# A decoder block on one core: products of the first up pair among those of the first gate pair, two products split by token tiles, and earlier loads in the down projection

## The chip, the core and the metric

The kernel runs on one core of a Trainium2 chip (trn2). The metric is the device time of one execution in microseconds, the median of the runs. Engines are named as in the profile: PE is TensorE's matmuls, PEld its weight loads, DVE is VectorE, ACT is ScalarE, POOL is GpSimd, and SP is SyncE, whose queue issues nearly all DMAs here.

## What is computed

One layer on 1024 tokens of width 1024: RMS norm, one input projection, a retention head group and a differential-attention head group, an output projection, and a SwiGLU feed-forward of width 2816. The change touches the part from the output projection on, which is:

```python
mix = jnp.concatenate([ret, dif.astype(ret.dtype)], axis=-1)
x = x + jnp.einsum('bse,ed->bsd', mix, w_out[l]).astype(x.dtype)

h2 = rms_norm(x, norm2_g[l])
ff = jax.nn.silu(jnp.einsum('bsd,df->bsf', h2, w_gate[l])) * jnp.einsum('bsd,df->bsf', h2, w_up[l])
x = x + jnp.einsum('bsf,fd->bsd', ff, w_down[l]).astype(x.dtype)
```

All in float32. To keep the precision, each product of two matrices is made of three matmuls on split operands: hi x hi, hi x lo and lo x hi, where hi is a value rounded to fp32r and lo is the rest (`mm3`).

## The kernel before

**Before the part in question.** Attention and retention run in steps over head groups and token tiles of 128, then the output projection (`o_proj`) of a token tile t and a half dh of the width, eight matmul triples each.

**The middle (`mid`, lines 1196 to 1216).** Thirteen output projections are still to be made (`PAIRS`), 104 steps of one triple, and then the first pair of gate columns, seven products of four steps each. In front of a pinned loop stands `MID_PLAN`, a list of (step, function, arguments) written out by hand: after a step's matmuls the functions of that step are called, and each engine runs its instructions in just that order. So MID_PLAN is the order of DVE, ACT and POOL in this stretch; PE's own order is that of the steps with the transposes between.

For each token tile t and half q of the width these functions follow one another:
- `o_add` (DVE) adds the projection to x, and SP stores the row to `x2d`; `n_square` (ACT) squares it with a sum; `n_rs` (POOL) makes the norm's factor; `n_scale` (DVE) scales the row in place; `n_turn` (PE) transposes it; `n_back` (ACT) copies it back, `n_hi` (ACT) and `n_lo` (DVE) split it.
- `f_sum` (DVE), `f_hi` (ACT), `f_lo` (DVE) make the sums and differences of such rows and split them.

The feed-forward's products are Strassen's: seven products n of quarter matrices in place of eight. The operand of product n from the tokens is a block `blk[b]` of four token tiles, and the seven products take b = 0, 3, 1, 4, 2, 5, 6 in this order. Block 0 holds tiles 0 to 3 of the first half of the width, block 3 the difference of the halves for them; block 1 holds tiles 4 to 7 of the second half, block 4 their difference, and 2, 5 and 6 mix both groups of tiles. `f_sum(b, p)` makes tile p of block b. So products 2 and 3 need token tile 7, the last one to come out of the output projection, as p = 3, and 4, 5 and 6 need all tiles.

The operand from the weights is `w_sum` (POOL, where the product takes a sum), `w_hi` (ACT) and `w_lo` (DVE), out of two raw halves that `Strassen.__init__` loads (tag rawp, three buffers, one of which holds the norm's gain `gtile` until the last `n_scale`). The first gate pair has these written into MID_PLAN as `gw_sum`, `gw_hi`, `gw_lo`; its results go out by `g_first` (ACT) and `g_more` (DVE). A product's bank in PSUM comes from three kinds, pp (two), m (two) and h (four), by `next_bank`.

**After the middle** nothing is pinned by hand: a scheduler sets the order of the up pair of the same columns and of ten more gate and up pairs. Each pair's planes go to DRAM (`ffd`, `plane`).

**The down projection** makes seven products n over 11 columns c. For each c it loads a plane into a ring of eight buffers (`a_load`), splits it and a weight (`operand`), and issues twelve matmuls, three into each of four banks. At the end of a product DVE adds the four banks to `acc` tiles, which `STARTS` loads from `x2d`: before the change in the last four columns of products 0 to 2, those of the half dh = 0 into the pool rowa, those of dh = 1 into rowb. rowa also holds the up results of the last pair until their planes are made, which `LAST` places at columns 3 to 7 of product 0.

In the notation below, g0 to g6 are the products of the first gate pair and u0 to u6 those of the first up pair.

Of the kernel before, what the change touches and what calls it, by code (L numbers as in the profile page):

```python
# [52 lines left out]
def constants():  # L53
# [69 lines left out]
    (0, "n_square", 1, 0),  # L123
# [6 lines left out]
    (1, "n_square", 0, 0),  # L130
# [97 lines left out]
    (80, "f_sum", 4, 1),  # L228
    (81, "o_add", 6, 0),
    (81, "f_hi", 4, 1),  # L230
    (82, "o_load", 7, 0),
    (82, "n_square", 6, 0),
    (82, "f_lo", 4, 1),
    (83, "n_lo", 5),
    (88, "o_add", 6, 1),
    (89, "gw_sum", 0),
    (89, "o_load", 7, 1),
    (89, "n_square", 6, 1),
    (90, "gw_hi", 0),
    (90, "n_rs", 6),  # L240
    (91, "gw_hi", 1),
    (91, "gw_lo", 0),
    (92, "gw_hi", 3),
    (92, "n_scale", 6, 0),
    (93, "gw_lo", 1),
    (94, "n_scale", 6, 1),
    (94, "n_turn", 6, 0),
    (95, "gw_lo", 3),
    (95, "n_back", 6, 0),
    (95, "n_turn", 6, 1),  # L250
    (95, "gw_sum", 2),
# [3 lines left out]
    (97, "f_sum", 4, 2),
    (98, "n_square", 7, 0),
    (98, "gw_lo", 2),
    (99, "gw_sum", 4),
    (99, "n_hi", 6),
    (100, "f_hi", 4, 2),  # L260
    (100, "n_lo", 6),
    (101, "gw_hi", 4),
    (101, "f_lo", 4, 2),
    (102, "gw_lo", 4),
    (103, "f_sum", 2, 0),
    (104, "gw_sum", 5),
# [1079 lines left out]
```

## Time and profile before

| | us |
|---|---|
| median of 3 runs | 1228.01 (1226.68 to 1230.36) |
| the profiled execution | 1226.93 |
| its span | 1225.1 |
| PE busy | 1204.8 |
| DVE busy | 838.1 |
| POOL busy | 570.8 |
| ACT busy | 537.2 |

The middle begins at about 503 us and the gate pair in it at 579.56; the down projection begins after 1005. A row of the timeline has the start, the time taken, the engine, the line, the operation with what it writes and reads, the shape, how many were merged, and in brackets the idle time of the engine before it with what ended it. Tile names come without numbers: in this stretch `x` is a token tile's row, `act` a block or the projection's operand, `whi` and `wlo` the weights' parts, `c` a result, `wide` a buffer of the down projection. All instructions of the pinned engines have the line of the helper, L347. A row of windows has the stretch, its length, the busy time and count of PE, PEld, DVE, ACT and POOL, the granted clock, the share of the DMA engines and GB/s.

### The profile page before, as it was taken

How to read it: one execution, taken by the hardware profiler on the slowest of the kernel's cores; microseconds unless marked ns; L12 is line 12 of the kernel's file. 1: busy time of each engine (PE TensorE's matmuls, PEld its weight loads, DVE VectorE, ACT ScalarE, POOL GpSimd, SP SyncE). 2: the span in 40 equal slices, each digit the busy share in tenths (PEclk: the TensorE clock that was granted, in tenths of full speed). 3: DMA queues.
4: the chain of work that ended last, by engine and by line, in shares of the span. 5: the costliest groups of instructions: out<-in, count | busy, mean ns of one | idle time of the engine just before them, and what ended most of it. 6: DMA issues, size and time to landing. Idle time of an engine off the chain costs nothing. (4 is left out here: it accounts for less than half of the span.)

```text
span 1225.1 us, 17316 instructions
## 1 busy us (share of the span) xinstructions
PE 1204.8 (98%) x5944; PEld 1020.6 (83%) x5944; DVE 838.1 (68%) x1491; ACT 537.2 (44%) x1194; POOL 570.8 (47%) x719
## 2 busy tenths in 40 slices
PE   8999999999999999999899999999999999999998
PEld 7898989888888888787688888888888888788887
DVE  6988888854444445545997665757657659698697
ACT  6856666643222224434544344333443434344442
POOL 2656555644444443102276456545566536154053
PEclk9999999999999999999999999999999999999999
DMA  6201011102111111422233333323334177943342
GB/s 201 67 21 32 27 30 35 44 17 88 52 35 40 39 35 45 154 84 72 60 122 119 95 103 112 128 71 103 104 112 129 69 254 247 349 144 99 95 116 83
DMA packets 97383, 117.34 MB, mean 96 GB/s; under 512 B 8976, under 2 KB 60304, under 8 KB 97296
## 3 DMA queue, kind: packets, MB, share of 16 engines
q1 hardware_dynamic: 95968, 115.65, 29.5%
q8 instruction: 47, 0.77, 0.3%
q10 hardware_dynamic: 1328, 0.60, 0.3%
q14 instruction: 40, 0.33, 0.1%
HBM read 87.64 MB, written 28.57 MB: 95 GB/s over the span
## 5 line engine op out<-in xcount | busy, mean ns | idle before, releaser
L347 PE MATMUL pp<-whi,act 128*128 128x384 f32 (+1 forms) x896 | 287.8, 373 | 0.7 <-ACT whi L347 0.7
L347 POOL TENSOR_TENSOR sum<-rawp 128x512 f32<-128x512 f32 x110 | 157.2, 1430 | 174.5 <-DVE wlo L347 152.6
L347 ACT CAST whi<-sum 128x512 fp32r<-128x512 f32 x165 | 102.6, 622 | 204.9 <-PE h L347 62.8
L347 DVE TENSOR_TENSOR wlo<-sum,whi 128x512 fp32r<-128x512 f32 x165 | 167.7, 1016 | 34.0 <-ACT whi L347 33.5
L347 PE MATMUL h<-act,whi 128*128 128x512 f32 x608 | 187.5, 389 | 0.3 <-DVE act L347 0.3
L347 PEld LDWEIGHTS pp<-whi,act 128*128 128x128 f32 x896 | 167.4, 189 | 15.2 <-ACT whi L347 1.0
L347 PE MATMUL pp<-wlo,act 128*128 128x384 f32 (+1 forms) x448 | 161.6, 361 | 0.6 <-DVE wlo L347 0.6
L347 POOL TENSOR_TENSOR sum<-wide 128x512 f32<-128x512 f32 x55 | 85.7, 1560 | 134.0 <-DVE wlo L347 101.9
L347 PEld LDWEIGHTS h<-act,whi 128*128 128x128 f32 x608 | 114.1, 188 | 24.5 <-DVE act L347 0.7
L347 PE MATMUL pp<-wrh,act 128*128 128x512 f32 x384 | 130.7, 402 | 0.0
L347 PE MATMUL h<-act,wlo 128*128 128x512 f32 x304 | 118.3, 389 | 0.0
L347 DVE TENSOR_TENSOR wlo<-wide,whi 128x512 fp32r<-128x512 f32 x99 | 78.5, 816 | 32.5 <-ACT whi L347 32.5
L347 PE MATMUL m<-act,whi 128*128 128x512 f32 x312 | 97.7, 394 | 1.8 <-ACT act L347 1.2
L347 ACT CAST whi<-wide 128x512 fp32r<-128x512 f32 x99 | 59.3, 620 | 87.3 <-PE m L347 48.0
L347 PE MATMUL pp<-act,whi 128*128 128x512 f32 x312 | 96.4, 390 | 0.7 <-DVE act L347 0.7
L347 PEld LDWEIGHTS pp<-wlo,act 128*128 128x128 f32 x448 | 85.1, 190 | 7.6 <-DVE wlo L347 1.2
L347 POOL TENSOR_TENSOR fsum<-c 128x512 f32<-128x512 f32 x55 | 79.2, 1451 | 11.0 <-DMA ffd<-fsum 11.0
L347 PEld LDWEIGHTS pp<-wrh,act 128*128 128x128 f32 x384 | 72.2, 188 | 14.3
L347 DVE TENSOR_TENSOR c<-c,h 128x512 f32<-128x512 f32 x88 | 58.1, 682 | 32.6 <-PE h L347 32.5
L347 DVE TENSOR_TENSOR wlo<-rawp,whi 128x512 fp32r<-128x512 f32 x44 | 47.4, 1077 | 41.1 <-ACT whi L347 40.2
L347 PE MATMUL pp<-wrl,act 128*128 128x512 f32 x192 | 74.8, 390 | 0.0
L347 PEld LDWEIGHTS m<-act,whi 128*128 128x128 f32 x312 | 59.2, 190 | 14.6 <-ACT act L347 1.4
(162 smaller groups left out, 2515.7 us busy)
## 6 DMA issues: line engine op xcount, KB each, us to landing
wide<-ffd SPq DMA_DIRECT2D x77, 256.0 KB, 2.7
ffd<-fsum SPq DMA_DIRECT2D x55, 256.0 KB, 2.0
rawp<-in_w_gate_dram SPq DMA_DIRECT2D x22, 512.0 KB, 3.8
rawp<-in_w_up_dram SPq DMA_DIRECT2D x22, 512.0 KB, 3.9
wide<-in_w_down_dram SPq DMA_DIRECT2D x44, 256.0 KB, 5.3
raw<-in_w_in_dram SPq DMA_DIRECT2D x32, 256.0 KB, 2.8
ffd<-c SPq DMA_DIRECT2D x22, 256.0 KB, 2.0
raw<-in_w_in_dram SPq DMA_DIRECT2D x26, 192.0 KB, 2.5
```

Of the source, the lines that this page charges most:

```text
L347: i = getattr(self.engine, op)(*args, **kw)
```

## The change

The up pair's first products come into the middle. `FIRSTS` sets PE's order: g0, g1, then g2 and g3 on the first three tiles of their blocks, then both on the last tile, then u0 to u3, g4 to g6 and u4 to u6. MID_PLAN is rewritten for it (a line or two are shown), with the functions taking the pair as their first argument; `u_load` loads the halves of up's raw weights. Three smaller edits go with it: the norm's mean is taken into the square's scale and its epsilon is added behind the first square of a tile, so that `n_rs` has two operations in place of three; the banks of the first 14 products are listed; and in the down projection the pools of `acc` change places, its loads go to the first four columns, and `LAST` starts a column later.

```diff
-    (95, "gw_sum", 2),
+    (111, "u_load", 0),
+    (119, "w_sum", 1, 0),
...
-        A.activation(sq, x2[t][i], AF.Square, accum_out=sums[t][:, i:i + 1])
+        A.activation(sq, x2[t][i], AF.Square, scale=D ** -0.5, accum_out=sums[t][:, i:i + 1])
+
+        if t not in eased:
+            eased.add(t)
+            G.tensor_scalar(sums[t][:, i:i + 1], sums[t][:, i:i + 1], EPS, None, op0=ALU.add)
...
-        G.tensor_scalar(ss2[:, 1:2], ss2[:, 0:1], 1.0 / D, EPS, op0=ALU.mult, op1=ALU.add)
-        rsqrt(ss2[:, 0:1], ss2[:, 1:2], 1)
+        rsqrt(ss2[:, 0:1], ss2[:, 0:1], 1)
...
+    FIRST_BANKS = "pmmphhhhpmmphh"
...
-        if 5 <= n_bank[0] <= 7 or n_bank[0] % 2 and n_bank[0] > 8:
-            return bankh()
-        return bankp() if n_bank[0] % 4 < 2 else bankm([P, 512])
+        kind = FIRST_BANKS[n_bank[0] - 1] if n_bank[0] <= len(FIRST_BANKS) else "phmh"[n_bank[0] % 4]
+        return {"h": bankh, "p": bankp, "m": lambda: bankm([P, 512])}[kind]()
...
-        def product(self, n):
-            hi, lo = self.w.pop(n)
+        def product(self, n, tiles=slice(0, 4)):
+
+            hi, lo = self.w.pop(n) if tiles.stop == 4 else self.w[n]
             b = blk[PRODUCTS[n][3]]
-            m = self.m[n] = next_bank()
+            if tiles.start == 0:
+                self.m[n] = next_bank()
+            m = self.m[n][:, tiles.start * P:tiles.stop * P]
             for k in range(4):
-                mm3(m, hi[:, k, :], lo[:, k, :], b[:, :, 0, k, :], b[:, :, 1, k, :], k == 0, k == 3)
+                mm3(m, hi[:, k, :], lo[:, k, :], b[:, tiles, 0, k, :], b[:, tiles, 1, k, :], k == 0, k == 3)
                 yield
...
+    ALL, HEAD, TAIL = slice(0, 4), slice(0, 3), slice(3, 4)
+    FIRSTS = [(0, 0, ALL), (0, 1, ALL), (0, 2, HEAD), (0, 3, HEAD), (0, 2, TAIL), (0, 3, TAIL),
+              (1, 0, ALL), (1, 1, ALL), (1, 2, ALL), (1, 3, ALL), (0, 4, ALL), (0, 5, ALL), (0, 6, ALL),
+              (1, 4, ALL), (1, 5, ALL), (1, 6, ALL)]
...
-        for n in range(7):
-            yield from gate[0].product(n)
+        for o, n, tiles in FIRSTS:
+            yield from firsts[o].product(n, tiles)
...
-            gate.append(Strassen(w_gate, 0, rowb, "rowb"))
+            firsts += [Strassen(w_gate, 0, rowb, "rowb"), Strassen(w_up, 0, rowa, "rowa", ())]
...
-        up = Strassen(w_up, f0, rowa, "rowa").whole()
+        up = Strassen(w_up, f0, rowa, "rowa").whole() if f0 else firsts[1].out
...
-    LAST = {3 + i: n for i, n in enumerate(n for n in range(7) if DOWN[n][0][1] is not None)}
+    LAST = {4 + i: n for i, n in enumerate(n for n in range(7) if DOWN[n][0][1] is not None)}
...
-            if n < len(STARTS) and c >= NH - 4:
-                t0 = c - NH + 4
+            if n < len(STARTS) and c < 4:
                 for sh, dh in STARTS[n]:
-                    t = 4 * sh + t0
-                    acc[t][dh] = (rowb if dh else rowa).tile([P, 512], F32, tag="rowb" if dh else "rowa", name="acc")
+                    t = 4 * sh + c
+                    acc[t][dh] = (rowa if dh else rowb).tile([P, 512], F32, tag="rowa" if dh else "rowb", name="acc")
```

What it does to the queues shows at three places. The first is PE at the end of g1. Before, the transposes of token tile 7 (`x2_6934` and `x2_6993`, its two halves) stand inside g1 (`m_7017`) and before g2 (`m_7065`), which takes 512 columns of block 1 (`act_6604`):

```order
L347 MATMUL m_7017<-act_6455,wlo_6899 128x512
L347 MATMUL h_7033<-cs_77,x2_6934 128x128 x4
L347 MATMUL m_7017<-act_6455,whi_6898 128x512 x2
L347 MATMUL m_7017<-act_6455,wlo_6899 128x512
L347 MATMUL h_7048<-cs_77,x2_6993 128x128 x4
L347 MATMUL m_7065<-act_6604,whi_6945 128x512 x2
```

Of the change, at the same place (tile 7 is `x2_6935` and `x2_6996`, g2 is `m_7056` and block 1 `act_6605`):

```order
L377 MATMUL m_7018<-act_6457,whi_6898 128x512 x2
L377 MATMUL m_7018<-act_6457,wlo_6899 128x512
L377 MATMUL h_7038<-cs_77,x2_6935 128x128 x4
L377 MATMUL h_7046<-cs_77,x2_6996 128x128 x4
L377 MATMUL m_7056<-act_6605,whi_6920 128x384 x2
L377 MATMUL m_7056<-act_6605,wlo_6921 128x384
```

Both transposes now stand behind all of g1, and g2 begins on three tiles, 384 columns.

The second is DVE from the addition of tile 7's second half on. Before (`sum` rows are `f_sum`, `act` from `sum` is `f_lo`, `act` from `h` is `n_lo`, the SCALAR_TENSOR_TENSOR is `n_scale`; blocks 2 and 5 are `act_6982` and `act_6983`):

```order
L347 TENSOR_TENSOR x2_6993<-pp_6937,xr_6882 128x512
L347 TENSOR_TENSOR act_6982<-sum_6985,act_6982 128x512
L347 TENSOR_TENSOR sum_7015<-x2_6409,x2_6697 128x512
L347 TENSOR_TENSOR sum_7021<-x2_6277,x2_6785 128x512
L347 SCALAR_TENSOR_TENSOR x2_6934<-x2_6934,sso_6953,gtile_6346 128x512
L347 TENSOR_TENSOR act_6983<-sum_7015,act_6983 128x512
L347 TENSOR_TENSOR sum_7038<-x2_6466,x2_6785 128x512
L347 TENSOR_TENSOR act_6982<-sum_7021,act_6982 128x512
L347 SCALAR_TENSOR_TENSOR x2_6993<-x2_6993,sso_6953,gtile_6346 128x512
L347 TENSOR_TENSOR act_6983<-sum_7038,act_6983 128x512
L347 TENSOR_TENSOR sum_7053<-x2_6331,x2_6874 128x512
```

Of the change (block 2 is `act_6984`, block 4 `act_6780`; `wlo` rows are `w_lo` of g5 and g6):

```order
L377 TENSOR_TENSOR x2_6996<-pp_6928,xr_6883 128x512
L377 TENSOR_TENSOR act_6780<-sum_6964,act_6780 128x512
L377 TENSOR_TENSOR sum_7009<-x2_6277,x2_6786 128x512
L377 TENSOR_TENSOR wlo_6990<-sum_6976,whi_6989 128x512
L377 SCALAR_TENSOR_TENSOR x2_6935<-x2_6935,sso_6948,gtile_6346 128x512
L377 SCALAR_TENSOR_TENSOR x2_6996<-x2_6996,sso_6948,gtile_6346 128x512
L377 TENSOR_TENSOR act_6984<-sum_6987,act_6984 128x512
L377 TENSOR_TENSOR sum_7054<-x2_6205,x2_6698 128x512
L377 TENSOR_TENSOR wlo_7032<-sum_7022,whi_7031 128x512
L377 TENSOR_TENSOR act_6984<-sum_7009,act_6984 128x512
```

The two scalings of tile 7 are neighbours now, and of blocks 2 and 5 only work on block 2 is left between.

The third is SP's queue in the first columns of the down projection. Before (`wide` from `ffd` is a ring load, `ffd` from `c` or `fsum` a plane's store):

```order
L1258 DMA ffd_195<-c_10458 128x512
L1249 DMA wide_10563<-ffd_195 128x512 x4
L1258 DMA ffd_195<-fsum_10690 128x512
L1249 DMA wide_10563<-ffd_195 128x512
L1258 DMA ffd_195<-fsum_10716 128x512
```

Of the change:

```order
L1309 DMA ffd_195<-c_10482 128x512
L1300 DMA wide_10587<-ffd_195 128x512 x3
L1361 DMA acc_10699<-x2d_194 128x512
L1361 DMA acc_10701<-x2d_194 128x512
L1300 DMA wide_10587<-ffd_195 128x512
L1361 DMA acc_10726<-x2d_194 128x512
L1361 DMA acc_10728<-x2d_194 128x512
```

Four of the eight acc loads of the first sum stand here now, ahead of the planes' stores; the other four stand ahead of all wide loads. Before, all eight came behind the fifth of these stores.

More of the change, by code (lines that the diff above doesn't have):

```diff
@@ L255 @@
[L255 to L266, printed above, removed]
+    (95, "w_lo", 0, 2),
+    (96, "w_hi", 0, 3),
+    (96, "o_add", 7, 0),
+    (96, "w_sum", 0, 4),
+    (96, "n_turn", 6, 1),
+    (97, "n_square", 7, 0),
+    (97, "w_lo", 0, 1),
+    (98, "n_back", 6, 1),
@@ new lines @@
+    (110, "n_scale", 7, 0),
+    (110, "w_hi", 0, 6),
+    (111, "n_scale", 7, 1),
+    (111, "n_turn", 7, 0),
+    (111, "f_lo", 2, 2),
+    (111, "u_load", 0),
+    (111, "n_turn", 7, 1),
+    (111, "n_back", 7, 0),
+    (111, "u_load", 1),
+    (111, "f_sum", 2, 0),
+    (112, "n_back", 7, 1),
+    (113, "w_lo", 0, 6),
+    (113, "f_hi", 2, 0),
+    (114, "f_lo", 2, 1),
+    (115, "n_hi", 7),
+    (115, "f_lo", 2, 0),
+    (117, "f_sum", 4, 3),
+    (118, "f_sum", 6, 0),
+    (118, "f_hi", 4, 3),
@@ new lines @@
+    (119, "n_lo", 7),
+    (119, "w_sum", 1, 0),
+    (119, "f_hi", 6, 0),
+    (120, "f_lo", 4, 3),
+    (121, "w_hi", 1, 0),
+    (123, "f_sum", 6, 1),
+    (123, "w_hi", 1, 1),
+    (125, "w_lo", 1, 1),
+    (125, "g_first", 0, 0),
+    (127, "w_lo", 1, 0),
+    (127, "f_hi", 6, 1),
+    (127, "f_lo", 6, 0),
+    (128, "f_lo", 6, 1),
+    (129, "f_sum", 5, 1),
+    (130, "f_sum", 5, 3),
+    (131, "f_hi", 5, 1),
+    (131, "w_sum", 1, 2),
+    (132, "f_hi", 5, 3),
+    (133, "w_sum", 1, 4),
@@ new lines @@
+    (133, "w_hi", 1, 2),
+    (134, "w_hi", 1, 3),
+    (135, "w_lo", 1, 2),
+    (135, "w_hi", 1, 4),
+    (135, "w_lo", 1, 3),
+    (136, "f_lo", 5, 3),
+    (137, "f_sum", 5, 0),
+    (138, "f_lo", 5, 1),
+    (139, "f_hi", 5, 0),
+    (139, "f_sum", 2, 3),
+    (139, "g_first", 1, 0),
+    (140, "f_lo", 5, 0),
+    (141, "f_hi", 2, 3),
+    (141, "f_sum", 5, 2),
+    (142, "f_lo", 2, 3),
+    (143, "f_hi", 5, 2),
+    (143, "f_sum", 6, 2),
+    (143, "g_first", 1, 1),
+    (144, "g_first", 1, 2),
@@ new lines @@
+    (144, "f_lo", 5, 2),
+    (145, "f_hi", 6, 2),
+    (145, "f_sum", 6, 3),
+    (146, "g_first", 0, 1),
+    (146, "f_lo", 6, 2),
+    (147, "g_first", 0, 2),
+    (147, "g_more", 0, 1),
+    (147, "w_sum", 1, 5),
+    (147, "f_hi", 6, 3),
+    (147, "g_more", 0, 2),
+    (148, "w_hi", 1, 5),
+    (148, "g_more", 0, 3),
+    (150, "f_lo", 6, 3),
+    (151, "w_lo", 1, 5),
+    (152, "w_lo", 1, 4),
+    (153, "g_more", 0, 4),
+    (153, "w_sum", 1, 6),
+    (155, "w_hi", 1, 6),
+    (155, "g_more", 1, 1),
@@ L330 @@
+    (156, "g_more", 1, 2),
+    (157, "g_more", 0, 5),
+    (158, "g_more", 0, 6),
+    (159, "w_lo", 1, 6),
+    (160, "g_more", 1, 3),
+    (162, "g_more", 1, 4),
+    (164, "g_more", 1, 5),
+    (167, "g_more", 1, 6),
 ]
@@ L1260, in block_kernel @@
     for f0 in range(0, NF, 2):
[L1261 removed]
+        g = Strassen(w_gate, f0, rowb, "rowb").whole() if f0 else firsts[0].out
         for g_ in g.values():
             A.activation(g_, g_, AF.Silu)
[L1264 removed]
+        up = Strassen(w_up, f0, rowa, "rowa").whole() if f0 else firsts[1].out
         if f0 == NF - 2:
```

224 lines of the change are left out of this document (91 added, 133 removed).

## The prediction

> **What bounds the kernel now.** I read the page first, then TensorE's waits, then the timeline around each wait.
>
> ```profile
> span 1225.1 us, 17316 instructions
> PE 1204.8 (98%) x5944; PEld 1020.6 (83%) x5944; DVE 838.1 (68%) x1491; ACT 537.2 (44%) x1194; POOL 570.8 (47%) x719
> 1052.78 1.36 PE pp L347 x6
> ```
>
> TensorE is busy for 98% of the span, and the chain that ended last is TensorE alone. Six 512-column matmuls take 1.36 us there, so one takes 0.2267 us and a product of twelve 2.72 us. The change takes no 512-column product away, so it can win only where TensorE stands still or runs at a reduced clock. The waits, cut into stretches, are these.
>
> ```profile
> 511.51 0.66 PE L347 MATMUL h<-cs,x 128*128 128x128 f32 x4 [1.18 <-DVE x L347]
> 559.31 0.63 PE L347 MATMUL h<-cs,x 128*128 128x128 f32 x4 [0.59 <-DVE x L347]
> 572.36 0.63 PE L347 MATMUL h<-cs,x 128*128 128x128 f32 x4 [0.38 <-DVE x L347]
> 579.56 0.61 PE L347 MATMUL pp<-act,whi 128*128 128x512 f32 x2
> 586.69 0.63 PE L347 MATMUL h<-cs,x 128*128 128x128 f32 x4 [1.06 <-DVE x L347]
> 588.48 0.49 PE L347 MATMUL m<-act,whi 128*128 128x512 f32 x1 [1.16 <-ACT act L347]
> 589.61 0.68 PE L347 MATMUL m<-act,whi 128*128 128x512 f32 x1 [0.63 <-DVE act L347]
> 594.94 0.50 PE L347 MATMUL pp<-act,whi 128*128 128x512 f32 x1 [0.66 <-DVE act L347]
> 606.34 0.62 PE L347 MATMUL pp<-act,whi 128*128 128x512 f32 x2
> 626.18 0.61 PE L347 MATMUL h<-act,whi 128*128 128x512 f32 x2
> 590.00:593.50 3.50, 3.50 (x10) 2.73 (x9) 3.47 (x3) 2.04 (x4) 3.27 (x3) 0.55 0.48 147
> ```
>
> Product 0 of the gate pair (g0) starts at 579.56, the first up product at 606.34, the next gate pair at 626.18. Between the first two stand 84 matmuls (19.04 us) and two groups of transposes of 0.36 us: 19.76 us of work in 26.78, so 7.0 us are lost. The waits name the cause: the transposes of token tile 7 wait for its scaling on DVE, then g2 and g3 for that tile's part of their operand. After the waits the granted clock (second last but one number of the last row) is 0.55 for 3.5 us. The up pair's 84 matmuls take 19.84 us instead of 19.04, another 0.8. The third place is the first sum of the down projection.
>
> ```profile
> 1042.38 0.39 PE L347 MATMUL pp<-whi 128*128 128x512 f32 x1
> 1045.65 0.50 PE L347 MATMUL pp<-wlo,whi 128*128 128x512 f32 x1 [2.89 <-DVE wlo L347]
> 1051.26 0.39 PE L347 MATMUL m<-whi 128*128 128x512 f32 x1
> DVE acc L347 <- DMA acc<-x2d: 3.2, 5, 0.7
> 1036.41 0.69 DVE L347 TENSOR_TENSOR acc<-acc,h 128x512 f32<-128x512 f32 x1 [0.44 <-PE h L347]
> 1043.71 1.28 DVE L347 TENSOR_TENSOR acc<-acc,h 128x512 f32<-128x512 f32 x2 [0.69 <-DMA acc<-x2d]
> 1044.91 7.68 DVE L347 TENSOR_TENSOR wlo<-wide,whi 128x512 fp32r<-128x512 f32 x9
> ```
>
> From 1042.38 to 1051.26 TensorE starts 18 matmuls, which need 4.08 us: 4.8 us are lost, 2.9 standing and the rest at the reduced clock. DVE made the eight additions of the first sum from 1036.41 to 1044.99 and stood 3.2 us in them, for the DMAs that bring acc; the weights' low parts were queued behind.
>
> **The change, part by part.** Times are on the clock of the profiled execution (1226.93 us, 1.8 more than its span).
>
> *Products in a new order.* 24 matmuls of 512 columns become 24 of 384 and 24 of 128. No row has an fp32r matmul of 128 columns, so I go by the nearest ones.
>
> ```profile
> 101.32 0.52 PE L347 MATMUL pp<-whi,act 128*128 128x384 f32 x2
> 102.39 0.34 PE L347 MATMUL pp<-whi,act 128*128 128x384 f32 x1
> 102.97 0.61 PE L347 MATMUL m<-v,aT 128*128 128x128 f32 x4
> 103.33 0.42 PE L347 MATMUL pp<-whi,act 128*128 128x384 f32 x1
> ```
>
> Six of 384 columns go from 101.32 to 102.39: 0.178 each. Four of 128 columns, each with weights of its own, take 0.36 us (102.97 to 103.33), 0.09 each. With 0.176 and 0.09 the 48 take 4.2 + 2.2 = 6.4 us where the 24 took 5.4: **1.0 us more**. Below, a third of the 384 columns' time is the least, 0.06, which makes it 0.2 more; above, the loads of weights (1020.6 us by 5944 on the page, 0.17 each) might not overlap, 0.17 each and 2.9 more, but then four of them would not go in 0.36. I take the row of four.
>
> [...]
>
> Without waits the two pairs take 144 matmuls at 0.2267 (32.6), two transposes (0.7) and 6.4: 39.7 us, against 46.6 between 579.56 and 626.18. So 6.9 us can be won at most. What waits are left, I walk through on DVE's new queue.
>
> ```profile
> 582.01 0.51 POOL L347 TENSOR_SCALAR sso<-sso 128x1 f32<-128x1 f32 x1
> 583.20 0.75 DVE L347 SCALAR_TENSOR_TENSOR x<-x,sso,gtile 128x512 f32<-128x512 f32 x1 [0.72 <-POOL sso L347]
> 545.59 1.42 DVE L347 SCALAR_TENSOR_TENSOR x<-x,sso,gtile 128x512 f32<-128x512 f32 x2 [2.03 <-POOL sso L347]
> 557.33 1.29 POOL L347 TENSOR_TENSOR sum<-rawp 128x512 f32<-128x512 f32 x1
> 557.40 2.43 DVE L347 SCALAR_TENSOR_TENSOR x<-x,sso,gtile 128x512 f32<-128x512 f32 x2 [1.37 <-POOL sso L347]
> 586.57 0.38 SPq L1108 DMA_DIRECT2D rawp<-in_w_up_dram  x1
> 590.60 3.14 POOL L347 TENSOR_TENSOR sum<-rawp 128x512 f32<-128x512 f32 x2 [0.23 <-DMA rawp<-in_w_up_dram]
> 590.95 1.65 DVE L347 TENSOR_TENSOR sum<-x,x 128x512 f32<-128x512 f32 x1
> 592.52 2.37 DVE L347 TENSOR_TENSOR act<-sum,act 128x512 fp32r<-128x512 f32 x2
> 599.56 0.69 DVE L347 TENSOR_TENSOR sum<-x,x 128x512 f32<-128x512 f32 x1
> 600.17 0.68 DVE L347 TENSOR_TENSOR act<-sum,act 128x512 fp32r<-128x512 f32 x1
> 618.51 1.56 DVE L347 TENSOR_TENSOR wlo<-sum,whi 128x512 fp32r<-128x512 f32 x1
> ```
>
> Back to back a DVE operation takes about 0.6 us (599.56 to 600.17). A weight sum on POOL beside it costs DVE about 1 us: two scalings take 1.42 alone and 2.43 beside one sum, and three operations took 3.9 us beside two. Step by step:
> - Tile 7's addition stays right behind o_proj's last product. POOL's chain for its norm let the scaling begin at 583.20; the scaled addition at 582.01 leaves it, 0.6 with the gap to the next, so the scaling can begin at 582.6. (It comes back as an addition behind tile 7's first square, between two gate sums, some 7 us earlier, where POOL waits for DVE's low part anyway.) The sum for g6 starts on POOL in the same moment, so the pair takes 2.43 and ends at 585.0 to 585.1. The transposes now stand behind g1, at 579.56 + 5.44 = 585.0: **a wait of about 0.1**.
> - The three-tile parts of g2 and g3 need nothing of tile 7: 585.7 to 590.0.
> - DVE does five operations to 588.0, then tile 7's difference for g3, one for g6, tile 7's low part for g2, and the low part for g3. Up's second raw half takes the buffer that the sum for g6 frees at 584.0 (in SP's queue both halves keep their places, around the last store); the DMA took 4.0 (586.57 to 590.6), so it lands at 588.0 and POOL runs two up sums beside just these operations. Three operations per 3.9 us then: g2's part is ready at 591.3, g3's at 592.2. The one-tile part of g2 would start at 590.0: **a wait of 1.2**; g3's doesn't wait.
> - up's first low part is done at about 594.0, u0 needs it then. u0 to u3 fill TensorE for 10.9 us, to 604.4. In that time DVE has 13 operations (7.9) with two POOL sums (2.0) beside them, and stands about 1 us behind ACT, whose queue has the casts of u2 and u3 behind two for g5: g4's last operand at 604.9, **a wait of 0.5**. g5 takes the bank of g1, which DVE's addition must have read: **0.4** more.
>
> Waits of 2.2 us: this part gains 6.9 - 2.2 = **4.7 us**; that the next pair then finds its weights ready follows from DVE's lead, since in the old order the low part of the next pair's first product was made at 618.51, some 7 us before 626.18.
>
> *Earlier steps of the same plan.* POOL now makes the first gate sum only behind tile 6's small addition, so it no longer meets the scaling at 557.40, and both turns of tile 6 stand later: of 0.59 and the 0.38 (with 0.1 behind it) I count **0.9 us** as gained. The 1.18 at 511 waits for a scaling that waits for the store of the row; nothing there moves.
>
> *The down projection.* acc's loads for the first sum go into the other row pool and to columns 0 to 3, four ahead of all wide loads and four between ring loads. DVE's eight additions then take 8 x 0.6 from 1036.41, to 1041.3, and the first low part is ready at 1042.0, 0.7 us before TensorE would run dry (1045.65 - 2.89): **4.8 us** gained. The sums that POOL makes for the last columns' planes come one column later, the same five of them, and the cover is the same. If a ring load slips by the 1 MB that is now ahead of it, it has eight columns of 2.72 us of lead. If the loads are late by more than 0.7 us in sum, what is beyond comes back as a wait.
>
> The sum: 4.7 + 0.9 + 4.8 = 10.4 us, so 1226.93 gives 1216.5. The profiled execution was 1.1 below the median of the runs, 1228.01, so I say **1217.5**.
>
> **The rivals.**
> 1. *DVE doesn't keep up, and the clock falls.* For it: DVE was busy 25.58 of the 26.80 us, and my walk leaves under 1 us of slack at four places. An idle of 1.18 (511) left the clock, idles of 2.9 within 4 us didn't. If the wait at the one-tile parts grows from 1.2 to 2.9, the reduced clock costs another 1.9 as at 590: the part keeps 1.1, the time is about 1221. [...]
> 2. *The down stall stays.* Another wait of the additions, for banks or for a late acc, takes its place: 10.4 - 4.8 leaves 5.6, about 1222.5. Against it: only 0.4 of the idle is TensorE's.
> 3. *Slower.* Up's second half has one buffer and the in-order queues of DVE and ACT put u0's weights ahead of g5's and g6's operands. From its landing to the low part are a POOL sum, a cast and a DVE operation, 1.3 + 0.6 + 0.7 with contention 3; u0 needs it at 594, so it may land until 591. Beyond that each us costs one, and 1.9 for the clock. It must land 8.5 us late, at 599.5, to undo all 10.4; the slowest rawp landing between 495 and 640 (last row below) took 8.7 us, which from 584 is 592.7. So 1230 needs a DMA of 15 us.
>
> ```profile
> 579.50:606.30 26.80, 23.03 (x93) 17.54 (x93) 25.58 (x38) 16.56 (x30) 7.28 (x7) 0.94 0.24 69
> DMA to landing us min/median/max: 3.5/3.9/8.7
> ```
>
> **How the numbers follow.** Both places as forecast: 0.61. Rival 1: 0.14. Rival 2: 0.10. Rivals 1 and 2 together, or gains that other waits eat: 0.10, within 0.3% (3.7 us, about what a measurement here can tell from no change). Slower: 0.05. The first three are faster by over 0.3%: 0.85. The range: no wait left and thin matmuls at 0.06 give 6.9 + 0.8 + 1.1 + 4.8 = 13.6, so 1214.4 from the median, and the fastest of the runs, 1226.68, lay 1.3 under it: 1213. At the other end it takes in rival 2: 1223.
>
> **What would show it.** Right: transposes of tile 7 with no wait over 0.3, a wait near 1.2 before the 128-column matmuls on m, none over 0.6 between up's products, about 42 us from g0 to the next pair, and acc additions without idle time for a DMA. Wrong: a granted clock near 0.55 in that stretch, g4 waiting over 2 us for its operand, u0 for its weights, or DVE idle in the first acc additions.

## The result and the profile after

| | us | ratio to the kernel before, 95% interval |
|---|---|---|
| before, 6 runs | 1228.30 (1226.68 to 1230.36) | |
| changed kernel, 6 runs | 1220.37 (1219.05 to 1223.85) | 0.9938 (0.9921 to 0.9956) |
| changed kernel on a second chip, 5 runs | 1219.35 (1218.07 to 1221.16) | 0.9927 (0.9913 to 0.9940) |
| profiled execution after, its span | 1223.85, 1222.0 | |

The changed kernel is faster by 8 to 9 us; 1217.5 was forecast, with 1213 to 1223 as the range. The profiled execution is the slowest of its six, so its profile shows what went wrong rather than what is usual. Its page:

```profile
span 1222.0 us, 17360 instructions
PE 1205.5 (99%) x5968; PEld 1024.6 (84%) x5968; DVE 834.7 (68%) x1491; ACT 536.7 (44%) x1194; POOL 571.1 (47%) x719
```

TensorE is busy for 99%, with 24 instructions more and 0.7 us more busy time than before: the 3 us of span came out of waits. All its waits over 0.25 us between 100 us and the end, and the rows at the cuts that are used below, stand in its timeline:

```profile
513.08 0.66 PE L377 MATMUL h<-cs,x 128*128 128x128 f32 x4 [1.40 <-DVE x L377]
579.68 0.62 PE L377 MATMUL pp<-act,whi 128*128 128x512 f32 x2
592.55 0.48 PE L377 MATMUL m<-act,whi 128*128 128x128 f32 x1 [2.16 <-DVE act L377]
627.24 0.62 PE L377 MATMUL h<-act,whi 128*128 128x512 f32 x2
1010.65 0.50 PE L377 MATMUL h<-whi 128*128 128x512 f32 x1 [0.41 <-DVE c L377]
```

The waits at tile 6's transposes (0.59 and 0.38 before), at tile 7's, at the undivided g2 and g3 and the 2.89 in the down projection are gone. What is left in the middle is one wait of 2.16 us, at the one-tile part of g2. The next rows are of the second chip's profiled execution (span 1217.6), at the same cuts:

```profile
512.50 0.66 PE L377 MATMUL h<-cs,x 128*128 128x128 f32 x4 [2.24 <-DVE x L377]
579.10 0.62 PE L377 MATMUL pp<-act,whi 128*128 128x512 f32 x2
591.97 0.33 PE L377 MATMUL m<-act,whi 128*128 128x128 f32 x1 [2.16 <-DVE act L377]
623.49 0.62 PE L377 MATMUL h<-act,whi 128*128 128x512 f32 x2
```

Cut at tile 0's transposes, at g0, at the next gate pair's first product and at the end, the three profiled executions (before: 511.51, 579.56, 626.18, 1225.1) give:

| stretch, us | before | after | after, second chip | forecast of the difference |
|---|---|---|---|---|
| start to tile 0's transposes | 511.51 | 513.08 | 512.50 | 0 |
| to g0 (o_proj) | 68.05 | 66.60 | 66.60 | -0.9 |
| g0 to the next gate pair | 46.62 | 47.56 | 44.39 | -4.7 |
| to the end (the down projection in it) | 598.92 | 594.76 | 594.11 | -4.8 |

The second line came better than forecast, and the last as forecast in one execution and 0.6 short of it in the other. The middle did not come as forecast: it lost 0.9 in one execution and won 2.2 in the other, with the same wait in both. The windows show what differs, the granted clock (second last number but one). These are of the first execution, cut where the clock's record changes:

```profile
589.01:592.42 3.41, 1.38 (x9) 1.18 (x7) 3.41 (x4) 1.11 (x2) 2.34 (x2) 1.00 0.08 29
592.42:595.83 3.41, 3.28 (x16) 3.28 (x16) 3.38 (x7) 2.65 (x6) 0.66 (x1) 0.50 0.00 0
595.83:599.25 3.42, 3.42 (x13) 3.12 (x13) 2.68 (x3) 1.31 (x3) 0.93 (x1) 0.50 0.00 0
599.25:602.66 3.41, 3.41 (x9) 2.64 (x8) 2.94 (x3) 1.48 (x3) 1.66 (x1) 0.50 0.00 0
602.66:606.00 3.34, 3.34 (x16) 2.69 (x15) 3.24 (x7) 2.11 (x4) 0.00 (x0) 1.00 0.49 157
```

From 592.42 to 602.66, three pieces of 3.413 us, TensorE ran at half clock, and in that time it did 23 of the 24 narrow matmuls and u0: 10.24 us for half as much work, so 5.1 us lost. In the second chip's execution the same record shows one such piece, 1.7 us lost. The pieces lie on a fixed grid of 3.413 us that runs through the whole record (its falls at 18.98 and 592.42 lie 168 periods apart), and its place against the wait differs: in the first execution a period ended at 592.42, 0.13 us before the matmul behind the wait, in the second chip's at 593.91, amid the narrow ones. So 47.56 = 40.3 of work + 2.2 of wait + 5.1 of clock, and 44.39 = 40.3 + 2.2 + 1.7 with 0.2 left over. The work itself is 144 matmuls at 0.2267 (32.6), transposes of 0.8, 24 of 384 columns at 0.1735 (4.2) and 24 of 128 at 0.111 (2.7; the spacing at full clock, from a run below).

Why the wait was 2.16 and not 1.2 stands on DVE and POOL, in the same profile after:

```profile
588.08 3.27 POOL L377 TENSOR_TENSOR sum<-rawp 128x512 f32<-128x512 f32 x2 [3.90 <-issue]
588.45 3.45 DVE L377 TENSOR_TENSOR sum<-x,x 128x512 f32<-128x512 f32 x2
591.82 0.68 DVE L377 TENSOR_TENSOR act<-h,act 128x512 fp32r<-128x512 f32 x1
```

Up's second raw half had landed and POOL had begun its two sums 0.37 us before DVE began tile 7's difference and the sum for g6. These two took 3.45 us beside them, and only then came tile 7's low part, at 591.82. The part for g2 was ready at 592.5; I had 591.3.

The down projection, DVE's row for the eight additions of the first sum, in the timeline after, and then the window around it:

```profile
1037.74 4.86 DVE L377 TENSOR_TENSOR acc<-acc,h 128x512 f32<-128x512 f32 x8
```

```profile
1036.00:1052.00 16.00, 16.00 (x72) 13.27 (x71) 14.83 (x23) 6.77 (x12) 3.39 (x2) 1.00 0.99 345
```

Eight additions in one piece, no DMA wait in them, TensorE without a pause and the clock at 1.00.

### The profile page after: what moved, and what is told of

Same layout as the page of the kernel before. It is cut to its first block, busy times and chain, and to the rows that moved or that the text cites. A ratio compares the mean times of both kernels' runs of the same rounds, so it can differ in the third digit from the quotient of the medians.

```text
span 1222.0 us, 17360 instructions
## 1 busy us (share of the span) xinstructions
PE 1205.5 (99%) x5968; PEld 1024.6 (84%) x5968; DVE 834.7 (68%) x1491; ACT 536.7 (44%) x1194; POOL 571.1 (47%) x719
## 4 chain that ended last, share of the span: by engine, by line
PE 93%; DVE 3%; DMA 2%; issue 1%; ACT 1%; POOL 0%; SPq 0%; ACTq 0%; DVEq 0%; POOLq 0%
PE pp L377 43%; PE h L377 27%; PE m L377 18%; PE big L377 3%; PE o L377 2%; PE it L377 1%; DMA wide<-in_w_down_dram 1%; DMA raw<-in_w_in_dram 1%; DVE act L377 0%; DMA x2d<-x 0%; DVE wlo L377 0%; DVE q L377 0%; DVE x L377 0%; SPq L1295 0%; DVE acc L377 0%
## 5 line engine op out<-in xcount | busy, mean ns | idle before, releaser
L377 DVE TENSOR_TENSOR wlo<-sum,whi 128x512 fp32r<-128x512 f32 x165 | 165.0, 1001 | 38.6 <-ACT whi L377 38.3
L377 PE MATMUL m<-act,whi 128*128 128x512 f32 (+2 forms) x320 | 98.3, 388 | 2.2 <-DVE act L377 2.2
L377 PE MATMUL pp<-act,whi 128*128 128x512 f32 (+2 forms) x320 | 98.1, 388 | 0.0
```

The source lines that it names most:

```text
L377: i = getattr(self.engine, op)(*args, **kw)
```

## The experiments

Each run stood against runs of the kernel before on its own chip, so ratios are compared, not times alone. The mean clock of an execution follows from how much of it ran at half clock; not all of that is the middle's, since nine of the fourteen profiled executions also have a piece of 3.41 us in their first 25 us, and a few have part of one at their very end.

**The two parts alone.** First the kernel before with the new loads of the down projection:

```diff
-            if n < len(STARTS) and c >= NH - 4:
+            if n < len(STARTS) and c < 4:
...
-                    acc[t][dh] = (rowb if dh else rowa).tile(...)
+                    acc[t][dh] = (rowa if dh else rowb).tile(...)
...
-    LAST = {3 + i: n ...}
+    LAST = {4 + i: n ...}
```

> The kernel before, with the down projection's part of the change alone. Theory (the down stall goes for good): DVE's eight additions of the first sum stand without idle time, TensorE shows no wait over 0.5 us and no reduced clock between 1036 and 1052, and the time is 4.0 to 4.8 us under the kernel before (the changed kernel gained 4.2 us between the second gate pair and the end). Rival (the stall only moves): another wait of over 2 us within 20 us of that place, and a time within 1 us of the kernel before.

Measured: 1224.13 us, ratio 0.9965 (0.9948 to 0.9981), so 4.3 us less with an interval of 2.3 to 6.4. DVE's rows in its timeline, and its window:

```profile
1037.80 4.86 DVE L347 TENSOR_TENSOR acc<-acc,h 128x512 f32<-128x512 f32 x8
1042.58 4.29 DVE L347 TENSOR_TENSOR wlo<-wide,whi 128x512 fp32r<-128x512 f32 x7
```

```profile
1036.00:1052.00 16.00, 16.00 (x73) 13.23 (x72) 14.63 (x23) 6.85 (x12) 3.07 (x2) 1.00 0.97 341
```

The stall goes and nothing takes its place. From the next gate pair (at 628.30) to the end of its span of 1222.4 this execution takes 594.1 us where the one before took 598.9: 4.8, the forecast. The second run is the changed kernel with these three edits undone:

> The changed kernel with the down projection as before. Theory A (the middle gains what was forecast, but the granted clock falls in some executions behind the 2.2 us wait of the first 128-column matmuls): the executions fall into two groups, some 4 to 5 us apart, those with the clock up 4 to 5 us under the kernel before, those with the clock down within 1 us of it; the wait of about 2 us stands in the trace either way. Rival B (the middle gains nothing): all executions within 1 us of the kernel before.

Measured: 1226.23 us, ratio 0.9979 (0.9962 to 0.9996). The twelve executions do not fall into two groups: their spans run from 1220.7 at a mean clock of 0.998 to 1228.3 at 0.991, one after the other. Neither theory had that, though A has the cause: the time goes with the clock. Its profiled execution has the 2.16 wait and one piece at half clock, from 595.1, behind most of the narrow matmuls; so it also shows their spacing at full clock, three in 0.33 us:

```profile
592.83 0.39 PE L377 MATMUL m<-act,whi 128*128 128x128 f32 x2
593.16 0.39 PE L377 MATMUL m<-act,whi 128*128 128x128 f32 x2
```

0.111 us each, not 0.09, and 0.213 at half clock (sixteen in the second window of the profile after). The whole division costs 24 x (0.1735 + 0.111 - 0.2267) = 1.4 us at full clock.

**Does the clock fall for the wait, or for the narrow matmuls?** First the 24 narrow matmuls were replaced, with the wait kept: the one-tile parts compute all four tiles again.

```diff
-    FIRSTS = [..., (0, 2, HEAD), (0, 3, HEAD), (0, 2, TAIL), (0, 3, TAIL), ...
+    FIRSTS = [..., (0, 2, HEAD), (0, 3, HEAD), (0, 2, ALL), (0, 3, ALL), ...
...
-            if tiles.start == 0:
+            if n not in self.m:
                 self.m[n] = next_bank()
```

> The changed kernel, whose one-tile parts of g2 and g3 compute all four tiles again (so three tiles of both are computed twice): the same wait ahead of them, but 24 matmuls of 512 columns behind it in place of 24 of 128. At full clock this is 24 x (0.2267 - 0.09) = 3.3 us more work, about 1 of which the later u0 may give back. Theory A (the narrow matmuls behind the wait hold the clock down for 10 us): the half clock lasts one piece of 3.4 us at most, and the stretch from g0 to the next gate pair takes 46 to 48 us, about that of the profiled changed kernel (47.6), in spite of the added work. Rival D (the wait alone sets how long the clock stays down): a half clock of about 10 us again, and a stretch of 50 to 51 us, a time 3 us over the changed kernel's.

Measured: 1220.73 us, ratio 0.9943 (0.9925 to 0.9961), the time of the changed kernel in spite of work that is 24 x (0.2267 - 0.111) = 2.8 us longer at full clock. The stretch took 47.04 us. The wait was 1.99 us, and behind it:

```profile
590.98:594.39 3.41, 1.42 (x6) 1.04 (x6) 3.38 (x5) 2.35 (x5) 0.99 (x1) 1.00 0.00 0
594.39:597.81 3.42, 3.42 (x9) 2.64 (x9) 3.42 (x5) 1.31 (x3) 1.59 (x1) 0.50 0.00 0
597.81:601.22 3.41, 3.41 (x16) 2.80 (x15) 2.20 (x5) 2.66 (x5) 0.10 (x1) 1.00 0.00 0
```

One piece, as theory A has it. But the changed kernel too shows one piece in some executions, so this alone does not settle it. Next the narrow part was made four times as long, once behind the wait and once on an order without one (that order is the second one below):

```diff
-            for k in range(4):
+            for k in range(4) if tiles.start == 0 else [0, 1, 2, 3] * 4:
                 mm3(m, hi[:, k, :], lo[:, k, :], ...)
...
```

> The changed kernel, whose one-tile parts of g2 and g3 are computed four times over (96 narrow matmuls in place of 24; the results are the same). In an earlier profile the narrow ones stood 0.111 us apart at full clock and 0.213 at half. Theory A (a wait of about 2 us brings the clock down, and narrow matmuls behind it hold it there until 512-column ones have filled a period of 3.4 us): half clock from the wait to 3 to 7 us behind the last narrow one, 20 to 27 us in all, in the executions in which it falls; the time is 12 to 16 us over the changed kernel's. Rival D (the wait alone decides, for 3.4 to 10.2 us): half clock for at most 10.2 us, a time of 8 to 11 us over the changed kernel's.

> As the run with four-fold narrow parts, but on the order with tile 7 and the weights first, so without the wait ahead of them. Theory A (narrow matmuls lower no clock without a wait): clock 1.00 from 579 to 640, 96 narrow matmuls in 10.7 us, a time 8.0 us over that of the order without repetition. Rival C (narrow matmuls alone bring the clock down): half clock from 3.4 to 6.8 us behind the first narrow one to their end and a little more, 14 us or more for the 96, a time 12 to 16 us over it.

Measured: 1235.78 us with the wait, ratio 1.0060 (1.0045 to 1.0074), all four executions at a mean clock of 0.990; 1224.20 without it, 0.9976 (0.9964 to 0.9988), at 0.996 to 0.999. That is 4.5 over the order without repetition, where 8.0 was expected: that order's wait of 2.30 at g5 (below), with the half clock behind it, is missing from this profile. With the wait, the clock was half in one piece of 20.48 us, from 593.4 to 613.9. The wait and DVE's and POOL's rows ahead of it in its timeline, then windows of the period before the fall, of three periods of narrow matmuls and of the last:

```profile
591.41 0.33 PE L377 MATMUL m<-act,whi 128*128 128x128 f32 x1 [1.10 <-DVE act L377]
588.37 2.38 DVE L377 TENSOR_TENSOR sum<-x,x 128x512 f32<-128x512 f32 x2
588.42 3.47 POOL L377 TENSOR_TENSOR sum<-rawp 128x512 f32<-128x512 f32 x2 [4.32 <-issue]
```

```profile
589.99:593.40 3.41, 2.31 (x21) 2.11 (x19) 3.38 (x5) 2.62 (x6) 1.89 (x2) 1.00 0.02 4
596.82:607.06 10.24, 10.24 (x50) 10.24 (x49) 5.57 (x8) 2.35 (x4) 1.27 (x1) 0.50 0.18 51
610.47:613.89 3.42, 3.42 (x10) 2.64 (x8) 1.39 (x2) 0.69 (x2) 0.00 (x0) 0.50 0.00 0
```

Without the wait, the same number of narrow matmuls filled whole periods at full clock:

```profile
591.58:594.99 3.41, 3.41 (x33) 3.41 (x32) 3.41 (x5) 2.18 (x4) 1.67 (x1) 1.00 0.00 2
594.99:598.41 3.42, 3.42 (x33) 3.42 (x32) 3.38 (x5) 2.12 (x4) 1.57 (x1) 1.00 0.00 0
```

So narrow matmuls of 128 columns do not bring the clock down, but hold it down. A count explains both. In 3.413 us at 0.2267 us for 512 columns, 7708 columns can stream. (The counts in brackets also take in matmuls that only end in a window; 30 or 31 of the narrow ones start in a period at full clock, 16 at half.) 31 x 128 are 0.51 of the 7708, and the clock stays up; at half clock 16 x 128 are 0.27, and it stays down; eight matmuls of 512 at half clock are 0.53, and it comes back. In the profile after, the first window before the fall has 0.35, the second of the three at half clock (seven narrow ones and four of 512) 0.38, the third 0.53. In the second chip's, the one period at half clock has 0.43, and the clock came back behind it. And a wait of only 1.10 us sufficed here, as narrow ones filled the rest of its period: 0.34. Over all profiled executions the middle's clock fell behind periods of 0.16 to 0.38.

The down projection shows the same without narrow matmuls. In the kernel before, its wait of 2.89 us brought the clock down; in the changed kernel with the old loads a longer one at the same place did not:

```profile
1043.96 0.50 PE L377 MATMUL pp<-wlo,whi 128*128 128x512 f32 x1 [3.30 <-DVE wlo L377]
1038.81:1042.23 3.42, 1.85 (x9) 1.20 (x7) 1.99 (x4) 1.14 (x2) 0.00 (x0) 1.00 1.06 403
1042.23:1045.64 3.41, 1.68 (x7) 1.42 (x8) 3.41 (x7) 0.00 (x0) 0.22 (x1) 1.00 1.05 386
```

Its 3.30 us fell into two periods, which by the count still streamed 0.50 and 0.45; before, the period from 1043.74 to 1047.15 streamed 0.40. So the length of a wait alone does not decide. The count is not sharp everywhere: in the first 20 us periods of 0.2 to 0.3 left the clock up in some executions and brought it down in others, and around tile 0's transposes, which I count at 128 columns each, periods of 0.37 to 0.41 left it up.

If this share decides, a wait is not needed at all; matmuls narrow enough bring the clock down by themselves. That was the next run, the order without a wait and 64-column matmuls:

```diff
-            for k in range(4):
-                mm3(m, hi[:, k, :], lo[:, k, :], b[:, tiles, 0, k, :], ...)
+            halves = [(0, P)] if tiles.start == 0 else [(0, 64), (64, P)] * 4
+            for i, (u, v) in enumerate(halves):
+                for k in range(4):
+                    mm3(m[:, u:v], hi[:, k, :], lo[:, k, :], b[:, tiles, 0, k, u:v], ...)
...
```

> The order with tile 7 first and no wait ahead of the narrow part, whose one-tile parts are made of matmuls of 64 columns, two for each tile and each four times over (192 in all; the results are the same). Over the traces so far, the share of full-rate columns that TensorE streams in a period of 3.413 us was 0.18 to 0.40 in the periods behind which the middle's clock fell, and 0.50 in those filled with 128-column matmuls, behind which it stayed. Theory G (that share of the period before decides): if the 64-column ones stand 0.08 to 0.111 us apart at full clock, the share is 0.26 to 0.36, and half clock begins 3.4 to 6.8 us behind the first of them, with no wait ahead, and lasts to their end; the time is 20 us or more over the run with 24 narrow ones. Rival H (only standing still lowers the clock): clock 1.00 throughout, 192 in 15 to 21 us.

Measured: 1250.88 us, ratio 1.0187 (1.0173 to 1.0201). There is no wait over 0.25 us behind 512, and:

```profile
590.91:594.33 3.42, 3.42 (x33) 3.42 (x33) 3.42 (x5) 1.77 (x4) 1.65 (x1) 1.00 0.00 0
594.33:621.63 27.30, 27.30 (x130) 27.30 (x130) 10.32 (x15) 4.48 (x8) 1.66 (x1) 0.50 0.06 20
625.05:628.46 3.41, 3.41 (x9) 2.64 (x9) 0.00 (x0) 0.30 (x1) 0.00 (x0) 0.50 0.00 0
```

30 of the 64-column matmuls start in the first window, a share of 0.25. The clock fell behind that period and stayed at half for 34.1 us, ten periods, with TensorE busy all the time by the profile's rows. So theory G holds here and rival H falls: in these runs the middle's clock goes by the share of streamed columns, 0.25 here with no idle stretch, 0.34 behind the wait of 1.10 us. At full clock 30 of these matmuls started in 3.35 us (589.10 to 592.45), about as close as the 128-column ones at 0.111; no run shows the 0.08 at the lower end of what was assumed. The pieces at half clock shown so far, of 3.41, 10.24, 20.48 and 34.1 us, are one, three, six and ten periods of 3.413.

**Can the wait be ordered away?** In this run DVE makes tile 7's difference for g3, its low part for g2 and the low part of that difference first:

```diff
+    (112, "f_lo", 2, 1),
     (113, "w_lo", 0, 6),
+    (113, "n_hi", 7),
+    (114, "f_sum", 4, 3),
+    (115, "n_lo", 7),
+    (115, "f_hi", 4, 3),
+    (116, "f_lo", 4, 3),
+    (117, "f_sum", 2, 0),
...
```

> The changed kernel, with tile 7's difference for g3, its low part for g2 and the low part of that difference put on DVE ahead of the sums and low parts for the fifth product, and up's first low parts right behind. Theory A (the wait of 2.2 us lets the clock fall, and the 128-column matmuls behind it hold it down for 10 us): no wait over 0.3 us ahead of the 128-column matmuls, they take about 0.09 each, the clock stays at 1.00 from 579 to 630, the stretch from g0 to the next gate pair takes 39.7 to 41 us instead of 47.6, and the time is 1215 to 1217.5 in every execution. Rival C (narrow matmuls alone bring the clock down): a half clock from about 590 on for 3 to 10 us without any wait, a stretch of 43 to 46 us, a time of 1219 to 1222.

Measured: 1222.87 us, ratio 0.9958 (0.9942 to 0.9975). No wait ahead of the narrow matmuls and no half clock there, as A has it; but the time did not come, since a new wait stood at u2, and the clock was half for 6.8 us from 600.44, within that wait, on:

```profile
602.30 1.22 PE L377 MATMUL h<-act,whi 128*128 128x512 f32 x2 [4.16 <-ACT whi L377]
```

The cast of u2's weights was queued on ACT behind casts that waited for DVE's sums, one at a time. So the weights of u1 to u3 went ahead, and DVE's sums in twos:

```diff
+    (118, "w_sum", 1, 2),
...
+    (120, "f_sum", 6, 0),
     (120, "w_hi", 1, 1),
+    (120, "w_hi", 1, 2),
     (121, "f_lo", 2, 0),
     (121, "w_lo", 1, 1),
     (121, "f_hi", 6, 0),
+    (121, "f_sum", 6, 1),
+    (122, "w_lo", 1, 2),
+    (122, "w_hi", 1, 3),
...
+    (124, "w_lo", 1, 3),
```

> Tile 7's work first on DVE as in the run before (whose new wait of 4.2 us stood at the third up product, for the cast of its weights, queued behind casts that waited for DVE's sums), and now the weights of the second to fourth up product ahead of the sums for g4 to g6, which go in twos. Theory A: no TensorE wait over 0.3 us between g0 and the next gate pair, clock 1.00 there, a stretch of 40 to 41 us (47.6 in the changed kernel's profile), and a time of 1214.5 to 1216.5 with little spread. Rival E (DVE's total work sets the pace, wherever tile 7 stands): a wait of 2 to 4 us comes back at g4, g5 or g6, a stretch of 43 us or more, a time of 1218 to 1221.

Measured: 1219.70 us, ratio 0.9929 (0.9915 to 0.9943), beside 0.9927 for the changed kernel in the same set of runs:

> The changed kernel itself, for the spread of its executions on the chip of the next three. Theory A (the time of an execution is a constant plus half the time at half clock): the spans of single executions follow their mean clock, about 1.2 us longer for each 0.001 of clock lost, between a span of 1217 at a clock of 0.999 or more and 1222 at 0.994; the profile shows one piece of 3.4, 6.8 or 10.2 us at half clock behind the wait of about 2.2 us, or none. Rival: spans that differ by 3 us or more at the same clock.

In this set the spans of the changed kernel's five executions ran from 1216.3 at a clock of 0.999 to 1219.4 at 0.996, none of them more than 1.3 us off another at the same clock. The reordered one gained nothing: rival E came true.

The wait in its timeline, and the window from tile 7's low part on:

```profile
608.80 0.73 PE L377 MATMUL m<-act,whi 128*128 128x512 f32 x2 [2.30 <-DVE c L377]
```

```profile
586.97:613.90 26.93, 24.63 (x118) 20.92 (x117) 26.49 (x37) 15.32 (x29) 8.41 (x6) 0.94 0.14 42
```

DVE is busy for 26.49 of 26.93 us, and g5 waited for the addition that reads its bank. The last step gives g5 the bank that only ACT reads and makes that addition ahead of g6's last low part:

```diff
-    FIRST_BANKS = "pmmphhhhpmmphh"
+    FIRST_BANKS = "pmmphhhhphmpmh"
...
+    (145, "g_more", 0, 1),
     (146, "g_first", 0, 1),
-    (146, "f_lo", 6, 2),
+    (146, "f_lo", 6, 3),
...
```

> The order with tile 7 and the up weights first, whose wait of 2.3 us stood at g5, for the addition on DVE that reads the bank g5 takes: g5 now takes the bank of u0, which ACT alone reads, the banks of u4 and u5 move with it, and DVE makes g1's addition ahead of the last low part for g6, ACT the casts for g6 ahead of the copies. Theory A: waits of at most 0.5 us between g0 and the next gate pair, clock 1.00 there, a stretch of 40 to 41 us, and a time of 1215.0 to 1217.0, some 3 us under the run it mends and the changed kernel. Rival E (DVE, busy without a gap from 587 to 613, sets the pace): waits of 1.5 us or more in sum at g5, g6 and u4, and a time within 1.5 us of the changed kernel's.

Measured: 1217.44 us (1216.64 to 1218.36), ratio 0.9913 (0.9900 to 0.9927). That is some 10 us under the kernel before, the fastest of all here; against the changed kernel's 0.9938 and 0.9927 the intervals overlap. Its waits and cuts:

```profile
579.61 0.61 PE L377 MATMUL pp<-act,whi 128*128 128x512 f32 x2
621.22 0.61 PE L377 MATMUL h<-act,whi 128*128 128x512 f32 x2
618.82 0.50 PE L377 MATMUL h<-act,wlo 128*128 128x512 f32 x1 [0.27 <-DVE wlo L377]
622.53 0.50 PE L377 MATMUL h<-act,wlo 128*128 128x512 f32 x1 [0.70 <-DVE wlo L377]
```

The stretch is 41.6 us, with no half clock in it; 40 to 41 was expected. What is left over 40.3 are small waits for low parts from DVE and, at g6, for a copy on ACT. The wait of 0.70 in the last row lies behind the cut, in the next gate pair.

**What is the division worth?** On that order, g2 and g3 were left undivided, in the place of their three-tile parts:

```diff
-    FIRSTS = [(0, 0, ALL), (0, 1, ALL), (0, 2, HEAD), (0, 3, HEAD), (0, 2, TAIL), (0, 3, TAIL), ...
+    FIRSTS = [(0, 0, ALL), (0, 1, ALL), None, None, (0, 2, ALL), (0, 3, ALL), ...
```

> The mended order (tile 7 first, other banks) with g2 and g3 undivided, in the place of their three-tile parts. Theory A (the division hides tile 7's way through ACT and DVE for 1.4 us of matmuls): waits of 2.2 to 2.6 us in sum at the first two matmuls of g2 (tile 7's high part at 587.2, its low part at 588.3, against 585.9), 1.4 us less of matmuls, so a stretch 1.0 us longer at full clock, and 1.7 more where a period with these waits streams under 0.40: 1.0 to 2.7 us over the mended order. Rival E (DVE sets the pace further on, so that the wait only comes out of later ones): the time within 0.5 us of the mended order, or under it.

Measured: 1218.43 us, ratio 0.9927 (0.9913 to 0.9940): by the ratios 1.7 us over the run it is compared with, which ran on another chip, and the intervals overlap. g2 waited 1.21 and 0.57 us, one piece at half clock followed, and the stretch took 42.9 us, 1.3 more than 41.6. That fits A, with a sum of waits of 1.8 where 2.2 was the least expected. At full clock the stretch would have been 1.7 shorter, so under that of the divided order: by this one pair of profiles, what the division buys is that the clock stays up.

**The norm's sums as before.** The edits of n_square and n_rs were undone in the changed kernel.

```diff
-        A.activation(sq, x2[t][i], AF.Square, scale=D ** -0.5, accum_out=sums[t][:, i:i + 1])
-        if t not in eased:
-            eased.add(t)
-            G.tensor_scalar(sums[t][:, i:i + 1], sums[t][:, i:i + 1], EPS, None, op0=ALU.add)
+        A.activation(sq, x2[t][i], AF.Square, accum_out=sums[t][:, i:i + 1])
...
-        rsqrt(ss2[:, 0:1], ss2[:, 0:1], 1)
+        G.tensor_scalar(ss2[:, 1:2], ss2[:, 0:1], 1.0 / D, EPS, op0=ALU.mult, op1=ALU.add)
+        rsqrt(ss2[:, 0:1], ss2[:, 1:2], 1)
```

> The changed kernel with the norm's sums as before (the scaled addition back in GpSimd's chain in front of the inverse root, none behind the squares). Theory A (that edit gives 0.6 us at tile 7's transposes, and the 0.6 and 0.4 in the o_proj stage by moving the first gate sum off tile 6's scaling): tile 7's scaling starts 0.6 us later against g0 than in the changed kernel, its transposes wait 0.5 to 0.7; the first gate sum stands at 557 again and the waits of 0.6 and 0.4 at 559 and 572 are back; 1.1 to 1.6 us over the changed kernel. Rival F (only the rows of the plan moved those waits): only the wait at tile 7's transposes comes, 0.5 to 0.7 us in all.

Measured: 1223.09 us, ratio 0.9958 (0.9945 to 0.9972), so 2.5 to 3.8 over the changed kernel; more than expected, but its profile also has 6.8 us at half clock and a mean clock of 0.994 to 0.997. The timelines of TensorE and POOL:

```profile
511.33 0.66 PE L377 MATMUL h<-cs,x 128*128 128x128 f32 x4 [1.22 <-DVE x L377]
559.17 0.63 PE L377 MATMUL h<-cs,x 128*128 128x128 f32 x4 [0.60 <-DVE x L377]
572.22 0.63 PE L377 MATMUL h<-cs,x 128*128 128x128 f32 x4 [0.38 <-ACT whi L377]
582.26 0.55 POOL L377 TENSOR_TENSOR sso<-sso,cs 128x1 f32<-128x1 f32 x1
```

The first gate sum stands at 557.18 again, and both waits in the o_proj stage are back; with g0 at 579.30 the stretch from tile 0's transposes takes 67.97 us, where the changed kernel takes 66.60 and the one before 68.05. So 1.37 of the 1.45 us gained there are this edit, and all the moved rows before it leave 0.1. DVE's scalings ahead of the first of the two waits, here and then in the changed kernel, show how:

```profile
557.25 2.43 DVE L377 SCALAR_TENSOR_TENSOR x<-x,sso,gtile 128x512 f32<-128x512 f32 x2 [1.38 <-POOL sso L377]
558.78 1.42 DVE L377 SCALAR_TENSOR_TENSOR x<-x,sso,gtile 128x512 f32<-128x512 f32 x2 [1.18 <-POOL sso L377]
```

Beside POOL's gate sum they take 2.43 us, without it 1.42. The 0.38 ends with a cast on ACT here and ended with DVE's scaling before, so its cause is not shown. At tile 7 the other half of theory A fell short: no wait over 0.25 came at its transposes, and the two groups took 1.05 us where the changed kernel's took 0.79. The inverse root on POOL, 0.55 in the last row of the first view, stands in the changed kernel's timeline as

```profile
582.03 0.89 POOL L377 TENSOR_TENSOR sso<-sso,cs 128x1 f32<-128x1 f32 x1
```

so of the 0.5 us saved by the missing addition, 0.34 went into a longer inverse root. Why it took longer is not shown: at the two tiles before, it took 0.56 and 0.57 us in the changed kernel and 0.55 and 1.01 here.

## Why the prediction was right, and where it was off

The sign and the time held: 1220.37 against 1217.5, inside the range. The mechanism held for the down projection and for o_proj, but not for the middle. Alone, the middle and o_proj gained 2.6 us by the ratio (0.5 to 4.7), where 4.7 + 0.9 was forecast. What happened there is rival 1, to which I gave 0.14 and about 1221: a longer wait for DVE, and the granted clock at half in that stretch, which I had named as a sign of being wrong. The time lies nearer to that rival's than to my own, and it is in the range because the range was wide enough for a loss of this size.

- **The down projection, 4.8 us: right.** 4.8 in two executions (598.92 to 594.1), 4.2 in the one profiled first, 4.3 as a ratio. Its mechanism held too, eight additions without a DMA wait; rival 2 fell.
- **o_proj, 0.9 us: right in cause, 1.45 in size.** Both waits went; the first by way of the first gate sum's place, as argued.
- **Waits left in the middle, 2.2 us: the sum right by luck, its parts not.** One wait of 2.16 stands for four that I had summed to 2.2. At tile 7's transposes there was none; those at g4 and g5 did not come, since TensorE was late by then. The one at g5 did come once the first was ordered away: 2.30, for the bank of g1, where I had 0.4.
- **The one-tile part of g2, 1.2 us: off by 1.0.** The step that failed is first my sum: at the rate that I name there, three operations in 3.9 us, a start at 588.0 gives 591.9 and a wait of 1.9, not 591.3 and 1.2. The rest is the start, 588.45, and 4.05 us for the three. In the run with four-fold narrow parts POOL began 0.05 us after DVE instead of 0.37 ahead, the first two operations took 2.38 us instead of 3.45, and the wait was 1.10. So both sizes are in the kernel, and a few tenths of a DMA's landing seem to choose; no run set that landing by itself.
- **Narrow matmuls, 0.09 us each: 0.111.** The division costs 1.4 us, not 1.0; the bounds 0.06 and 0.17 held it.
- **The clock: left out of the sum, and the main error.** I priced it in rival 1 alone, for a wait of 2.9, at 1.9 us. It fell at 2.16 and cost 5.1 in the first execution and 1.7 in the second chip's, as the narrow matmuls behind the wait hold it down: 16 of them, 0.27 of the columns, filled the period from 592.42, and the clock stayed at half. What fills the period that a wait has begun was the question to ask.
- **Not in the sum: the start.** The 1.0 to 1.6 us that both executions after came later to tile 0's transposes are no part of the change; over the profiled executions of these runs, whose code up to there differs by next to nothing, that row stands anywhere from 511.3 to 513.7. Why is open.

Summed for the second chip's execution: 1.0 - 1.45 - 2.2 - 4.8 = -7.5, its span against that of before (1217.6 and 1225.1).

## What to carry to other kernels

A wait on TensorE is priced with what runs behind it: narrow matmuls after a short wait can cost more in clock than the wait itself (5.1 us against 2.16 here), so the pieces of a divided product belong where no wait stands ahead of them (four times as many: ratio 1.0060 behind the wait, 0.9976 on an order without one), or, as an estimate from the count of columns that no run tried, behind wide ones. When an order is changed to remove one wait, count the busy time of the engine that feeds it: at 26.5 of 27 us the next wait is already there, and moving work about only moves it; here other banks for two products and an earlier addition took it away (a stretch of 41.6 us, with the wait 44.6). A single profiled execution can be the worst of its kernel; a second one and the mean clocks of all runs tell which part of it is usual.

## What the runs showed of the hardware

- From 520 us on, TensorE's clock fell to half behind periods of 3.413 us in which 0.40 or less of the full-rate columns streamed, and stayed up or came back behind those with 0.43 or more. This held also where TensorE was never idle: 30 matmuls of 64 columns in a period (0.25) brought it down, 30 of 128 (0.50) did not. A wait of 3.30 us that fell into two periods (0.50 and 0.45) left it up. In the first 20 us and around the fp32 transposes at 511 us the share does not part the two cases.
- An fp32r matmul of 64 columns, with weights of its own, takes as long as one of 128: 0.111 us at full clock and 0.213 at half (128 of 64 columns start in 27.30 us). From 128 to 64 columns nothing is won.
- The same two additions on DVE took 3.45 us when POOL's sums began 0.37 us earlier, and 2.38 when they began 0.05 us later.
